# Loading positions as four rows and ordering the rotary angles around a transposed gain column

## The chip, the cores and the metric

The kernel runs on one core of one Trainium2 chip, as one launch. The metric is the device time in microseconds (us), lower is better. The engines are named as in the profile: PE is TensorE (PEld its weight load), DVE is VectorE, ACT is ScalarE, POOL is GpSimd, SP is SyncE; a q behind a name (SPq) is that engine's instruction queue where it issues a DMA.

## The reference

Two layers over 512 tokens of width 1024, all in float32. The first is a dilated attention mixer with three groups of heads, the second an mLSTM mixer; each is followed by a SwiGLU block, and a last norm ends it. What the change touches is the start of the first layer: the norm of `x`, the projections of queries and keys, and the rotary angles.

```python
def rms_norm(x, g):
    xf = x.astype(jnp.float32)
    y = xf * lax.rsqrt(jnp.mean(xf * xf, axis=-1, keepdims=True) + RMS_EPS)
    return y.astype(x.dtype) * g.astype(x.dtype)

def apply_partial_rope(t, positions):
    half = ROT_DIM // 2
    inv_freq = ROPE_THETA ** (-jnp.arange(half, dtype=jnp.float32) * 2.0 / ROT_DIM)
    ang = positions.astype(jnp.float32)[..., None] * inv_freq
    cos, sin = jnp.cos(ang)[:, :, None, :], jnp.sin(ang)[:, :, None, :]
    ...

def dilated_attention_mixer(xn, positions, w_in, w_out):
    proj = (xn @ w_in).reshape(B, S, N_GROUPS, 3, ATTN_HEADS, ATTN_HEAD_DIM)
    for g, (window, dilation) in enumerate(DIL_CONFIGS):
        q = apply_partial_rope(proj[:, :, g, 0], positions) * scale
        k = apply_partial_rope(proj[:, :, g, 1], positions)
        ...
```

`positions` is one row of 512 int32.

## The kernel before, in words

Activations lie with features on the 128 partitions and the 512 tokens along the free axis, in eight tiles. Every matmul operand is split into a high part in the reduced type `float32r` and the remainder as a low part, and three products (high times high, high times low, low times high) take the place of one full-precision product. ACT makes the high part, DVE the low part. Weights come in chunks of 512 KB on SP's DMA queue through three buffers.

The order at the start is written out by hand. The helper `behind(fn, ..., engine=E)` (L389) places what `fn` issues behind the last instruction so far on engine E, and `both` (L442) behind the last on ACT and on DVE; they set the order in which the program is laid out on each engine, and each engine then works through its own list in that order. The waits between engines follow from the data alone. The start is, in the order of the code:

- L93 to L108: constants (`cst`: identity, inverse frequencies, signs) are loaded on SP, the first norm's gains as eight rows (`attn_rows`) on POOL; DVE fills `ones`, `ones_r` and `idle_w`; PE runs nine matmuls on them (`idle(9)`) whose result is never read.
- L109, L110: ACT loads the table of the sine by a dummy activation (`warm`).
- L335 to L341: `posi` holds the positions of tokens c, c+4, c+8, ... on partition 32c, for c from 0 to 3, 128 numbers each. POOL fills the tile with 0; then four DMAs bring one row each, c = 0 and 1 issued by ACT, c = 2 and 3 by SP (L379). Each takes every fourth of the 512 integers.
- L375 to L383, on SP: four times a quarter of `x` (`x_tok`, 512 KB), and a quarter of the first weights (`first_w`, 256 KB), then two more blocks of constants. The two position DMAs stand behind the first quarter of `x`.
- `gains` (L401): PE transposes the gains (`arT`), DVE copies them to columns (`cols`).
- `rope_angles` (L346): DVE casts `posi` to `n`, spreads each partition 32c over 32 partitions (`stream_shuffle`), multiplies by the inverse frequencies, takes off whole turns (a rounding by adding and subtracting a large number, then three fused steps with a three-part two pi), and clips: nine instructions.
- `x_quarter(q)` (L446): PE transposes two tiles of `x` into PSUM (`xT`); ACT makes the high part `xa_h` with the gain as its scale (it reads `cols`), DVE the low part `xa_l`.
- `rope_tables` (L357): ACT takes the sine of the angle and of its half, DVE forms the signed sine and the cosine, POOL copies them into `sinn` and `cosn` in eight pieces. They are read by `rope_scale` (L505).
- `first_split(q)` (L416): ACT and DVE split a quarter of the first weights (`first_h`, `first_l`); `first_mm(q)` (L421) is the twelve matmuls on it.
- `x_keep` (L406): copies of the transposed `x` into the residual `h`; `squares` (L434): ACT's sums of squares for the norm.

The order in the code is: gains, angles, `x_quarter(0)`, tables, `first_split(0)`, four more idle matmuls, `first_mm(0)`, `x_keep(0)`, `x_keep(1)`, `first_split(1)`, `x_quarter(1)`, `x_quarter(2)`, `first_split(2)`, `first_mm(1)`, and so on to the ordinary loop over pairs of heads (`attention_pair`, L529, with `project`, L246).

Of the kernel before, what the change touches and what calls it, by code (L numbers as in the profile page):

```python
# [11 lines left out]
F32 = mybir.dt.float32  # L12
F32R = mybir.dt.float32r
I32 = mybir.dt.int32
AF = mybir.ActivationFunctionType
ALU = mybir.AluOpType
AX = mybir.AxisListType
P = 128

SEQ = 512  # L20
# [50 lines left out]
def tile_hybrid_dilated_attn_mlstm(  # L71
# [4 lines left out]
    nc = tc.nc  # L76
# [3 lines left out]
    def pool(stack, name, **kw):  # L80
        return stack.enter_context(tc.tile_pool(name=name, bufs=1, **kw))

    cp = pool(ctx, "const")
# [12 lines left out]
    ones = cp.tile([P, 1], F32, name="ones")  # L96
# [8 lines left out]
    def idle(n):  # L105
        for i in range(n):
            nc.tensor.matmul(idle_ps, ones_r, idle_w, start=True, stop=True)
    idle(9)  # L108
    warm = cp.tile([P, 1], F32, name="warm")  # L109
    nc.scalar.activation(warm, ones[:, 0:1], AF.Sin)  # L110
    cols = cp.tile([P, 80], F32, name="cols")
    rows = cp.tile([80 - KC, P], F32, name="rows")
    row_of = {"attn": 0}
# [45 lines left out]
    def last_on(engine):  # L159
        for ins in reversed(nc.cur_bb.bb.instructions):  # L160
            if ins.engine == engine:
                return ins
# [161 lines left out]
    with ExitStack() as actx:  # L324
        ap = pool(actx, "attn")
# [6 lines left out]
        cosn = ap.tile([R, SEQ], F32, name="cosn")  # L332
        sinn = ap.tile([R, SEQ], F32, name="sinn")
        sinr = ap.tile([R, SEQ], F32, name="sinr")
        posi = ap.tile([P, P], I32, tag="rt", name="posi", bufs=2)  # L335
        nc.gpsimd.memset(posi, 0)

        def load_positions(queue, cs):
            for c in cs:
                queue.dma_start(posi[32 * c:32 * c + 1], positions.rearrange("o (j c) -> c o j", c=4)[c])  # L340
        load_positions(nc.scalar, (0, 1))  # L341

        tmp = ap.tile([P, 2, SEQ], F32, tag="vf", name="angles")
        ang, n, sn, cs = (tmp[:, 0, i * P:(i + 1) * P] for i in range(4))

        def rope_angles():  # L346

            nc.vector.tensor_copy(n, posi)
            nc.vector.stream_shuffle(ang, n, [0] * 32)
            nc.vector.tensor_scalar(ang, ang, cst[:, K_INV:K_INV + 1], None, op0=ALU.mult)  # L350
            nc.vector.tensor_scalar(n, ang, 1.0 / TWO_PI, ROUND, op0=ALU.mult, op1=ALU.add)
            nc.vector.tensor_scalar(n, n, ROUND, None, op0=ALU.subtract)
            for c in (C1, C2, C3):
                nc.vector.scalar_tensor_tensor(ang, n, -c, ang, op0=ALU.mult, op1=ALU.add)
            nc.vector.tensor_scalar(ang, ang, math.pi, -math.pi, op0=ALU.min, op1=ALU.max)
# [19 lines left out]
        for q in range(4):  # L375
            nc.sync.dma_start(xtok[:, :, q * 256:(q + 1) * 256],
                              x.rearrange("(j c) d -> j c d", c=4)[:, :, q * 256:(q + 1) * 256])
            if q == 0:
                load_positions(nc.sync, (2, 3))  # L379
            nc.sync.dma_start(piece(raws, q).rearrange("p (k n) -> p k n", k=2),  # L380
                                w_in[q * 256:(q + 1) * 256, 0:256].rearrange("(k p) n -> p k n", p=P))
        nc.sync.dma_start(acst, consts[:, K_MA:])
# [6 lines left out]
        def behind(fn, *args, engine=mybir.EngineType.PE):  # L389

            with tc.issue_after(last_on(engine)):
                fn(*args)
# [47 lines left out]
        ACT, DVE = mybir.EngineType.Activation, mybir.EngineType.DVE  # L440

        def both(fn, *args):  # L442
            with tc.issue_after(last_on(ACT)):
                behind(fn, *args, engine=DVE)

        def x_quarter(q):  # L446
            for k in (2 * q, 2 * q + 1):
                behind(x_in, k)
        behind(gains)
        rope_angles()  # L450
        both(x_quarter, 0)
        behind(rope_tables, engine=ACT)
        both(first_split, 0)
        behind(idle, 4)
        behind(first_mm, 0)
        both(x_keep, 0)
        both(x_keep, 1)
        both(first_split, 1)
        x_quarter(1)
        x_quarter(2)  # L460
        both(first_split, 2)
# [385 lines left out]
    with ExitStack() as mctx:  # L847
# [53 lines left out]
        for p_ in (0, 32):  # L901
            s = slice(p_, p_ + H)
# [54 lines left out]
        for b in range(TB):  # L957
            s = slice(32 * b, 32 * b + H)
# [155 lines left out]
    with ExitStack() as fctx:  # L1114
# [22 lines left out]
        for n in range(2):  # L1137
# [29 lines left out]
            for at, tb, cs in tiles:  # L1167
# [12 lines left out]
                if n == 1 and cs.stop == 512:  # L1180
# [4 lines left out]
                    r = fr[:, tb:tb + 1]  # L1185
# [34 lines left out]
```

## Time and profile before

| what | us |
|---|---|
| median of 3 runs | 1482.64 |
| lowest and highest run | 1482.47, 1483.17 |
| the profiled execution | 1482.45 |
| its span | 1480.7 |
| its mean PE clock over the span | 0.998 |

The profile is of one execution. In a line of the timeline the first number is the start in us from the start of the span, the second how long the instruction, or the run of instructions merged into the line (x and their count), took; then engine, source line, operation, and the tiles written and read; in square brackets how long the engine had stood idle, and what released it. The end of a matmul is modelled, and one begins before the last has ended: the step from start to start is what tells PE's pace. In a row of stretches the first number behind the window is its length, then the busy time of PE, weight load, DVE, ACT and POOL with their instruction counts, the granted PE clock as a share of full, the busy share of the 16 DMA engines, and GB/s. A DMA row gives the size and the us from the issue to the landing.

### The profile page before, as it was taken

Reading aid. Unit: us, or ns where it says so; the run is one execution under the profiler, and the core shown is the slowest. Engines: PE = TensorE matmul, PEld = TensorE weight load, DVE = VectorE, ACT = ScalarE, POOL = GpSimd, SP = SyncE. Lnnn points to the kernel's source line nnn. Section 1 sums busy time; section 2 is a strip of 40 time slices with the busy share of each in tenths; the row PEclk is TensorE's granted clock in tenths of the full one; section 3 lists DMA queues with packets and bytes.
Section 4 is the critical chain, followed back from the end, with each engine's and each line's share of the span. In section 5 each row is a group of like instructions: output and inputs, shape, how many; then the busy total and the mean of one; then the engine's idle time right before and its main releaser. Section 6 shows DMA issues by size and latency. Waiting matters only on the chain. (4 is left out here: it accounts for less than half of the span.)

```text
span 1480.7 us, 18935 instructions
## 1 busy us (share of the span) xinstructions
PE 1469.2 (99%) x7497; PEld 1254.1 (85%) x7497; DVE 768.1 (52%) x1511; ACT 544.7 (37%) x997; POOL 104.4 (7%) x96
## 2 busy tenths in 40 slices
PE   9999999999999999999999999999999999999998
PEld 7899889889889888888888889798888888888887
DVE  6754654654665363343443338987755443443233
ACT  5334225225226342232332223785543333233223
POOL 1000000000000000111110000000000111110011
PEclk9999999999999999999999999999999999999999
DMA  6322222232132223333323333131233333333231
GB/s 185 99 86 72 82 90 72 81 92 85 58 100 80 78 86 100 100 100 100 91 88 105 94 93 88 58 100 58 74 112 92 93 99 100 100 89 96 85 100 72
DMA packets 129033, 134.45 MB, mean 91 GB/s; under 512 B 6000, under 2 KB 122032, under 8 KB 128944
## 3 DMA queue, kind: packets, MB, share of 16 engines
q1 hardware_dynamic: 126672, 131.55, 28.9%
q8 instruction: 59, 0.97, 0.3%
q10 hardware_dynamic: 1936, 1.12, 0.2%
q0 software_dynamic: 336, 0.57, 0.1%
q14 instruction: 30, 0.25, 0.1%
HBM read 131.12 MB, written 2.10 MB: 90 GB/s over the span
## 5 line engine op out<-in xcount | busy, mean ns | idle before, releaser
L241 PE MATMUL f0j<-n_h,f0j_h 128*128 128x512 f32 x352 | 137.1, 389 | 0.0
L241 PE MATMUL f1j<-n_h,f1j_h 128*128 128x512 f32 x352 | 137.1, 389 | 0.0
L241 PE MATMUL f0j<-n_h,f0j_l 128*128 128x512 f32 x352 | 137.0, 389 | 0.0
L241 PE MATMUL f1j<-n_h,f1j_l 128*128 128x512 f32 x352 | 137.0, 389 | 0.0
L241 PE MATMUL f0j<-n_l,f0j_h 128*128 128x512 f32 x352 | 136.9, 389 | 0.0
L241 PE MATMUL f1j<-n_l,f1j_h 128*128 128x512 f32 x352 | 136.9, 389 | 0.0
L211 DVE TENSOR_TENSOR f1j_l<-f1j_w,f1j_h 128x1024 fp32r<-128x1024 f32 x44 | 54.9, 1247 | 54.5 <-ACT f1j_h L210 54.5
L211 DVE TENSOR_TENSOR f0j_l<-f0j_w,f0j_h 128x1024 fp32r<-128x1024 f32 x44 | 54.8, 1245 | 54.5 <-ACT f0j_h L210 54.5
L241 PEld LDWEIGHTS f1j<-n_l,f1j_h 128*128 128x128 f32 x352 | 66.1, 188 | 13.8
L241 PEld LDWEIGHTS f0j<-n_h,f0j_h 128*128 128x128 f32 x352 | 66.1, 188 | 13.8
L241 PEld LDWEIGHTS f0j<-n_l,f0j_h 128*128 128x128 f32 x352 | 66.1, 188 | 13.7
L241 PEld LDWEIGHTS f1j<-n_h,f1j_h 128*128 128x128 f32 x352 | 66.1, 188 | 13.8
L241 PEld LDWEIGHTS f0j<-n_h,f0j_l 128*128 128x128 f32 x352 | 66.1, 188 | 13.6
L241 PEld LDWEIGHTS f1j<-n_h,f1j_l 128*128 128x128 f32 x352 | 66.1, 188 | 13.6
L210 ACT ACTIVATE f1j_h<-f1j_w 128x1024 fp32r<-128x1024 f32 x44 | 46.5, 1057 | 73.3 <-PE f1j L241 72.2
L210 ACT ACTIVATE f0j_h<-f0j_w 128x1024 fp32r<-128x1024 f32 x44 | 46.5, 1057 | 73.3 <-PE f0j L241 72.2
L1152 PE MATMUL fin<-fw_h,f1ah 128*128 128x512 f32 (+1 forms) x198 | 72.8, 368 | 0.0
L1152 PE MATMUL fin<-fw_l,f1ah 128*128 128x512 f32 (+1 forms) x198 | 72.5, 366 | 0.0
L1152 PE MATMUL fin<-fw_h,f1al 128*128 128x512 f32 (+1 forms) x198 | 72.4, 366 | 0.0
L241 PE MATMUL fo<-f0ah,fo_k_h 128*128 128x512 f32 x176 | 68.5, 389 | 0.0
L241 PE MATMUL fo<-f0al,fo_k_h 128*128 128x512 f32 x176 | 68.5, 389 | 0.0
L241 PE MATMUL fo<-f0ah,fo_k_l 128*128 128x512 f32 x176 | 68.5, 389 | 0.0
(1167 smaller groups left out, 3582.3 us busy)
## 6 DMA issues: line engine op xcount, KB each, us to landing
f0j_w<-in_ffn_w_in_dram SPq DMA_DIRECT2D x44, 512.0 KB, 3.6
f1j_w<-in_ffn_w_in_dram SPq DMA_DIRECT2D x44, 512.0 KB, 3.5
fw_w<-in_ffn_w_out_dram SPq DMA_DIRECT2D x22, 512.0 KB, 3.8
fo_k_w<-in_ffn_w_out_dram SPq DMA_DIRECT2D x20, 512.0 KB, 3.5
awo_k_w<-in_attn_w_out_dram SPq DMA_DIRECT2D x8, 512.0 KB, 3.4
mv_k_w<-in_mlstm_w_in_dram SPq DMA_DIRECT2D x8, 512.0 KB, 3.7
mqk_k_w<-in_mlstm_w_in_dram SPq DMA_DIRECT2D x8, 512.0 KB, 3.6
mo_k_w<-in_mlstm_w_in_dram SPq DMA_DIRECT2D x8, 512.0 KB, 3.7
```

The lines of the kernel that those rows point to most:

```text
L210: nc.scalar.activation(hi[:, :n], raw[:, :n], AF.Copy)
L211: nc.vector.tensor_tensor(lo[:, :n], raw[:, :n], hi[:, :n].bitcast(F32), op=ALU.subtract)
L241: nc.tensor.matmul(acc, whl[a][:, k, m * P:(m + 1) * P], pairs[b][kk], start=(kk == 0 and (a, b) == SPLITS[0]), stop=(kk == nk - 1 and (a, ...
L1152: nc.tensor.matmul(acc[i][:, cs], a[a_][kk][:, tb * P:(tb + 1) * P], whl[b_][:, k, cs], start=(kk == 0 and (a_, b_) == SPLITS[0]), stop=(k ...
```

## The change

The positions come in by one DMA that ACT issues as its first instruction: the whole row of 512 integers, four times, onto partitions 0, 32, 64 and 96. POOL's fill of the position tile goes; DVE fills the float tile `n` with 0 instead, and four casts of one partition each pick every fourth integer. The dummy sine follows the DMA on ACT.

The nine angle instructions are cut in two. `rope_turns` (zero fill, casts, shuffle, the multiplication by the frequencies, the division into turns with the rounding constant) is placed ahead of `gains`, so that on DVE it stands before the copy of `cols`; the rest, `rope_angles`, follows that copy. `rope_tables` moves from behind `x_quarter(0)` to behind `first_split(1)`.

On the engines that gives: PE, the same instructions in the same order. DVE, `memset n` behind the first memset and ahead of `ones_r`; four casts, shuffle and two scalings ahead of `cols`; the three operations of the tables behind the second `first_l` instead of ahead of the first. ACT, the DMA first of all, and the two sines behind the second `first_h` instead of ahead of the first. POOL, one memset less. SP, two DMAs less between the first quarter of `x` and the first quarter of the weights.

```diff
@@ -106,8 +106,6 @@
     idle(9)
-    warm = cp.tile([P, 1], F32, name="warm")
-    nc.scalar.activation(warm, ones[:, 0:1], AF.Sin)
     cols = cp.tile([P, 80], F32, name="cols")
@@ -332,23 +330,25 @@
-        posi = ap.tile([P, P], I32, tag="rt", name="posi", bufs=2)
-        nc.gpsimd.memset(posi, 0)
-
-        def load_positions(queue, cs):
-            for c in cs:
-                queue.dma_start(posi[32 * c:32 * c + 1], positions.rearrange("o (j c) -> c o j", c=4)[c])
-        load_positions(nc.scalar, (0, 1))
-
+
+        posi = ap.tile([P, SEQ], I32, tag="rt", name="posi", bufs=2)
+        nc.scalar.dma_start(posi.rearrange("(c r) s -> c r s", c=4)[:, 0], positions[0:1].to_broadcast([4, SEQ]))
+        warm = cp.tile([P, 1], F32, name="warm")
+        nc.scalar.activation(warm, ones[:, 0:1], AF.Sin)
         tmp = ap.tile([P, 2, SEQ], F32, tag="vf", name="angles")
         ang, n, sn, cs = (tmp[:, 0, i * P:(i + 1) * P] for i in range(4))
 
-        def rope_angles():
-
-            nc.vector.tensor_copy(n, posi)
+        def rope_turns():
+
+            nc.vector.memset(n, 0.0)
+            for c in range(4):
+                s = slice(32 * c, 32 * c + 1)
+                nc.vector.tensor_copy(n[s], posi[s].rearrange("p (j c) -> p c j", c=4)[:, c])
             nc.vector.stream_shuffle(ang, n, [0] * 32)
             nc.vector.tensor_scalar(ang, ang, cst[:, K_INV:K_INV + 1], None, op0=ALU.mult)
             nc.vector.tensor_scalar(n, ang, 1.0 / TWO_PI, ROUND, op0=ALU.mult, op1=ALU.add)
+
+        def rope_angles():
             nc.vector.tensor_scalar(n, n, ROUND, None, op0=ALU.subtract)
             for c in (C1, C2, C3):
                 nc.vector.scalar_tensor_tensor(ang, n, -c, ang, op0=ALU.mult, op1=ALU.add)
@@ -375,8 +375,6 @@
-            if q == 0:
-                load_positions(nc.sync, (2, 3))
@@ -446,16 +444,18 @@
-        behind(gains)
-        rope_angles()
+        rope_turns()
+        with tc.issue_after(last_on(DVE)):
+            behind(gains)
+        behind(rope_angles, engine=DVE)
         both(x_quarter, 0)
-        behind(rope_tables, engine=ACT)
         both(first_split, 0)
         behind(idle, 4)
         behind(first_mm, 0)
         both(x_keep, 0)
         both(x_keep, 1)
         both(first_split, 1)
+        both(rope_tables)
         x_quarter(1)
```

## The prediction

> **What bounds the kernel now.** I read the page's first part, then every wait of TensorE (PE) over the span, then the first 35 us in order of time, and last busy time by stretches. The profiled execution took 1482.45 us: a span of 1480.7 and 1.75 around it. The median of the runs, 1482.64, is 0.19 above it.
>
> ```profile
> span 1480.7 us, 18935 instructions
> PE 1469.2 (99%) x7497; PEld 1254.1 (85%) x7497; DVE 768.1 (52%) x1511; ACT 544.7 (37%) x997; POOL 104.4 (7%) x96
> ```
>
> PE is busy for 99% of the span, so the change can count only where PE stands still or runs slowly. All waits of PE (us in total, times, longest):
>
> ```profile
> PE a0g0q L428 <- ACT first_h L418: 1.9, 1, 1.9
> PE idle L107 <- DVE idle_w L102: 1.5, 1, 1.5
> PE m0s L1035 <- DVE ks L1007: 0.7, 1, 0.7
> PE m0s L1035 <- DVE m0e L1037: 0.6, 1, 0.6
> ```
>
> The change reaches the first: the first real matmul (L428) waits 1.9 us for ScalarE's (ACT's) first weight split (L418). The path to it, in order of time (start, us, engine):
>
> ```profile
> 5.66 0.27 PE L403 MATMUL arT<-cst,attn_rows 8*128 8x8 f32 x1
> ...
> 7.01 1.51 ACT L228 ACTIVATE xa_h<-xT,cols 128x512 fp32r<-128x512 f32 x2 [4.78 <-PE xT L284]
> ...
> 9.26 0.23 DVE L355 TENSOR_SCALAR angles<-angles 128x128 f32<-128x128 f32 x1
> 9.40 1.40 DVE L229 SCALAR_TENSOR_TENSOR xa_l<-xT,cols,xa_h 128x512 fp32r<-128x512 f32 x2
> ...
> 9.52 0.31 ACT L358 ACTIVATE angles<-angles 128x128 f32<-128x128 f32 x1 [1.00 <-DVE angles L355]
> 9.94 0.61 ACT L418 ACTIVATE first_h<-first_w 128x512 fp32r<-128x512 f32 x1
> 10.60 0.50 PE L428 MATMUL a0g0q<-xa_h,first_h 128*128 128x512 f32 x1 [1.88 <-ACT first_h L418]
> ...
> 11.38 0.69 DVE L419 TENSOR_TENSOR first_l<-first_w,first_h 128x512 fp32r<-128x512 f32 x1
> ...
> 15.14 1.91 PE L284 MATMUL xT<-cst,x_tok 128*128 128x128 f32 x16
> ```
>
> ACT is free at 7.01 + 1.51 = 8.52, but its next instruction in order is the sine (L358), which waits 1.00 us for the last angle on VectorE (DVE); the split stands behind it. PE's twelve matmuls then fill 10.60 to 15.14, 4.54 us. That they also run slowly is seen in stretches of 3.41 us (length; PE busy; weight load, DVE, ACT, POOL; then PE clock, DMA share, GB/s):
>
> ```profile
> 7.67:11.08 3.41, 1.53 (x7) 0.97 (x7) 3.20 (x11) 2.27 (x6) 0.02 (x1) 1.00 1.01 338
> 11.08:14.49 3.41, 3.41 (x10) 2.30 (x9) 2.75 (x6) 0.00 (x0) 3.10 (x8) 0.50 1.07 358
> 14.49:17.90 3.41, 3.38 (x24) 2.79 (x22) 1.40 (x3) 2.12 (x4) 0.17 (x1) 1.00 0.95 305
> 949.76:953.17 3.41, 2.79 (x13) 1.98 (x11) 3.32 (x6) 3.40 (x12) 0.61 (x1) 1.00 0.01 2
> 1471.95:1475.36 3.41, 2.23 (x19) 2.03 (x17) 2.04 (x9) 1.64 (x5) 1.66 (x3) 1.00 0.34 125
> 1475.36:1478.77 3.41, 0.00 (x0) 0.00 (x0) 1.10 (x5) 0.93 (x2) 0.63 (x1) 1.00 0.37 141
> 1478.77:1480.70 1.93, 0.00 (x0) 0.00 (x0) 0.00 (x0) 0.00 (x0) 0.00 (x0) 0.50 0.20 77
> ```
>
> The granted clock is exactly halved from 11.08 to 14.49, the stretch that follows one in which PE was busy for only 1.53 of 3.41 us. After stretches with 2.79 and 2.23 us busy it stays whole; after an empty one at the end it halves again. So in this trace the clock is set by stretches of 3.41 us, and the bound for halving lies between 1.53 and 2.23 busy.
>
> **The change part by part.** The program's order on PE is the same before and after; DVE gets one memset and three casts more, POOL one memset less, SP two DMAs less, ACT one DMA less.
>
> *The memset of n* now stands on DVE ahead of the idle weights, so PE's idle block and all behind it (arT, transposes, xa_h) start later. Nothing covers that: PE runs that block without a gap to arT. The row of a memset on DVE and of a 128x128 operation there (below) bound it:
>
> ```profile
> 0.74 0.39 SPq L93 DMA_DIRECT2D cst<-in_shape_constants_dram  x1
> 0.81 0.06 DVE L97 MEMSET ones<- 128x1 f32 x1 [0.81 <-PEq L1209]
> ...
> 6.84 0.23 DVE L348 CAST angles<-posi 128x128 f32<-128x128 int32 x1 [0.70 <-DMA posi<-in_positions_dram]
> 7.11 0.30 DVE L349 STREAM_SHUFFLE angles<-angles 128x128 f32<-128x128 f32 x1
> 7.44 0.28 DVE L350 TENSOR_SCALAR angles<-angles,cst 128x128 f32<-128x128 f32 x1
> 7.76 0.23 DVE L351 TENSOR_SCALAR angles<-angles 128x128 f32<-128x128 f32 x1
> 8.02 0.23 DVE L352 TENSOR_SCALAR angles<-angles 128x128 f32<-128x128 f32 x1
> ```
>
> 0 (hidden in the wait for the first memset) to 0.23; I take 0.10, nearer the memset.
>
> *The positions.* One DMA on ACT, without POOL's memset to wait for, is ACT's first instruction, so at about 0.74 like SP's first. The table load follows it; ACT has nothing else to do before 7.01, which covers both. Landing, by the nearest rows (the last number: us from issue to landing):
>
> ```profile
> attn_rows<-in_attn_norm_dram POOLq DMA_DIRECT2D x1, 4.0 KB, 3.1
> posi<-in_positions_dram ACTq DMA_DIRECT2D x1, 0.5 KB, 3.7
> first_w<-in_attn_w_in_dram SPq DMA_DIRECT2D x1, 256.0 KB, 4.6
> ```
>
> Landed at 3.8 to 4.4, and with 0.2 for the waking of DVE usable at 4.0 to 4.6. The four-row form is not in the trace; the far bound is the 4.6 of a transfer that queues, usable at 5.5. Behind this wait stand, on DVE, the casts, shuffle, two scalings, then cols (L404) and everything after it, and so ACT's xa_h, which reads cols. Four casts at a step of about 0.15 (no row has a one-row cast; 0.23 each at most), then steps of 0.33, 0.32 and 0.26 read from the rows above: cols can run 1.65 us after the positions are usable, 5.65 to 6.25. It needs arT anyway, which ends at 5.93 + 0.10 = 6.03; ACT needs cols at 7.11. Cost 0. After cols the other five angle operations take 1.5 (8.02 to 9.49 now), so the angles end at 7.7 to 7.9, just when the first xa_h does (7.01 + 0.69 + 0.10 = 7.80): xa_l is not held. It would be from about 4.6 on, and the low weight part at PE from about 4.9; later positions cost their delay, 0.6 at the far bound.
>
> *The split ahead of the sines.* xa_h ends at 8.62. The split's start against that end, its lead to PE's start, and PE's pace at full clock:
>
> ```profile
> 3.51 0.59 SPq L380 DMA_DIRECT2D first_w<-in_attn_w_in_dram  x1
> ...
> 20.72 0.48 PE L428 MATMUL a0g0q<-xa_h,first_h 128*128 128x512 f32 x1
> 21.03 0.40 PE L428 MATMUL a0g0q<-xa_l,first_h 128*128 128x512 f32 x1
> 21.05 1.27 ACT L228 ACTIVATE xa_h<-xT,cols 128x512 fp32r<-128x512 f32 x2
> 21.26 0.39 PE L428 MATMUL a0g0q<-xa_h,first_l 128*128 128x512 f32 x1
> 22.19 0.65 ACT L418 ACTIVATE first_h<-first_w 128x512 fp32r<-128x512 f32 x1
> ```
>
> There the split starts 0.13 before xa_h ends (21.05 + 1.27 against 22.19), so here at 8.49. Its weights land today at 3.51 + 4.6 = 8.1, and will land earlier with two DMAs gone from in front of them on SP. PE starts 0.66 later (10.60 - 9.94): 9.15 in place of 10.60, **1.45 us**. First use of xa_l: ready at 8.6. DVE: second xa_l from 8.66, the low part (L419) 0.66 later at about 9.3, done 10.0; PE wants it as fifth matmul at 9.15 + 0.31 + 3 x 0.23 = 10.15. No stall, 0.15 to spare.
>
> *The clock.* The idle matmuls end at 8.72 + 0.10 (of the 1.53 busy after 7.67, 0.48 lie behind 10.60), so PE now stands for about 0.3 us, not 1.9, and the stretch 7.67 to 11.08 is busy for 3.1, far over the 2.23 that kept the clock. Twelve matmuls at full clock take 0.31 + 11 x 0.228 = 2.82 instead of 4.54: **1.72 us**. The second transposes begin at 11.97 instead of 15.14.
>
> [...]
>
> *The moved sines.* On ACT (two sines), DVE (three operations, 0.7 us) and POOL (eight copies) they follow the second split, into time in which ACT and DVE wait for the second transposes. Their reader is late:
>
> ```profile
> 33.38 0.67 DVE L506 TENSOR_TENSOR sinr<-xbc,sinn 32x512 f32<-32x512 f32 x1
> ```
>
> and PE is busy throughout the stretch after the start:
>
> ```profile
> 30.00:100.00 70.00, 70.00 (x332) 58.82 (x331) 51.03 (x97) 20.59 (x35) 0.00 (x0) 1.00 0.32 98
> ```
>
> DVE ends h, h and the second low part at about 11.8 and the three by 12.5; the next xa_l needs a transposed tile (11.97 + 4 x 0.12) and 0.69 of xa_h behind it, so it cannot start before 13.1. Cover 0.6; without it their 0.7 would be on the path. POOL ends near 16, the reader comes near 30. Later loads are issued earlier too, as their buffers come free, so all behind moves with the transposes; PE has no gap there to take the gain back (70.00 of 70.00).
>
> **Sum.** 1.45 + 1.72 = 3.17, the memset's 0.10 taken off (2.4 to 3.3 with the bounds of memset and positions): 1482.45 - 3.17 = 1479.3, and by the runs' median 1479.5. That is 0.21%; 0.2% (3.0 us, about what a measurement of this kernel can tell from no change) lies just inside.
>
> **Rivals.** [...] *Positions somewhat late*, usable at 4.9 to 7.0: gain between 3.2 and nothing, middle 1481.0. *Slower: positions so late that DVE's new place makes cols the last event.* Point of decision: usable at 7.0, when cols ends at 8.8, both xa_h at 10.1, PE starts at 10.66 with the gap and the halved clock back. Each us more costs one; at a landing of 7.4 us, twice today's 3.7, they are usable at 8.3: 1483.9. Against: no small transfer took over 3.7. *The edit doesn't take effect*: the first weights, not the sine, hold ACT until 9.9; 1482.6. Against: their 4.6.
>
> **How the numbers follow.** Forecast 0.72, clock 0.10, late positions 0.08, slower 0.05, no effect 0.03, a gain over 3.5 us 0.02. Of the forecast's own range, 1479.2 to 1479.9, three quarters lie beyond 0.2%: faster 0.55 + 0.02 = 0.57; slower by over 0.2% 0.03, as it needs positions some 9 us late or another stall of that size; the rest, 0.40, within. The range 1478.8 to 1481.5 takes in the forecast, the clock and half of late positions.
>
> **What would show it.** Right: first L428 near 9.15 after a wait near 0.3; clock 1.00 in all stretches to 20 us; second transposes near 12.0; cols by 6.3; sines without a wait. Wrong: cols or xa_l waiting for the positions' DMA; first split waiting for its DMA; matmuls at 0.43; a new PE wait before 35 us.

## The result and the profile after

The changed kernel takes 1479.6 us (median of 15 runs, 1478.86 to 1479.93), the kernel before, in the same comparison, 1482.74 (15 runs, 1481.47 to 1483.65). The ratio is 0.9979, with a 95% interval of 0.9971 to 0.9987: 3.14 us or 0.21% faster. The profiled execution of the changed kernel took 1479.76, its span 1478.0.

The page's first part for the changed kernel: PE is as full as before, and its busy time is 1.4 us less for the same 7497 matmuls.

```profile
span 1478.0 us, 18932 instructions
PE 1467.8 (99%) x7497; PEld 1253.0 (85%) x7497; DVE 769.0 (52%) x1515; ACT 544.9 (37%) x997; POOL 103.4 (7%) x95
```

All waits of PE in it (us in total, times, longest). The first real matmul now waits 0.4 us instead of 1.9; the other three rows are those of before to within 0.1.

```profile
PE idle L107 <- DVE idle_w L102: 1.5, 1, 1.5
PE m0s L1035 <- DVE ks L1007: 0.7, 1, 0.7
PE m0s L1035 <- DVE m0e L1037: 0.7, 1, 0.7
PE a0g0q L426 <- ACT first_h L416: 0.4, 1, 0.4
```

The start in order of time. The positions are issued first of all and usable at 2.77; the angles are done at 7.50, ahead of the first `xa_l` (7.73); ACT goes from `xa_h` straight into the split (8.45); PE begins at 9.12 and then works without a gap to the second transposes at 11.99. The two sines (9.49 to 9.99) wait for nothing.

```profile
0.74 1.10 ACTq L335 DMA_DIRECT2D posi<-in_positions_dram  x1
2.77 1.10 DVE L346 CAST angles<-posi 1x128 f32<-1x128 int32 x4 [1.30 <-DMA posi<-in_positions_dram]
5.65 0.27 PE L401 MATMUL arT<-cst,attn_rows 8*128 8x8 f32 x1
5.96 0.17 DVE L402 COPY cols<-arT 128x8 f32<-128x8 f32 x1 [1.15 <-PE arT L401]
7.27 0.23 DVE L355 TENSOR_SCALAR angles<-angles 128x128 f32<-128x128 f32 x1
7.73 1.60 DVE L227 SCALAR_TENSOR_TENSOR xa_l<-xT,cols,xa_h 128x512 fp32r<-128x512 f32 x2 [0.23 <-ACT xa_h L226]
8.45 1.14 ACT L416 ACTIVATE first_h<-first_w 128x512 fp32r<-128x512 f32 x2
9.12 0.50 PE L426 MATMUL a0g0q<-xa_h,first_h 128*128 128x512 f32 x1 [0.35 <-ACT first_h L416]
9.25 0.68 DVE L417 TENSOR_TENSOR first_l<-first_w,first_h 128x512 fp32r<-128x512 f32 x1
9.49 0.30 ACT L358 ACTIVATE angles<-angles 128x128 f32<-128x128 f32 x1
10.17 0.40 PE L426 MATMUL a0g0q<-xa_h,first_l 128*128 128x512 f32 x1
11.99 1.91 PE L282 MATMUL xT<-cst,x_tok 128*128 128x128 f32 x16
```

The same stretches as before the change (length; PE, weight load, DVE, ACT, POOL; clock, DMA share, GB/s). The clock is whole in the stretch in which it was halved:

```profile
7.67:11.08 3.41, 3.06 (x13) 2.19 (x13) 3.25 (x6) 2.15 (x6) 0.00 (x0) 1.00 1.09 359
11.08:14.49 3.41, 3.39 (x23) 2.83 (x22) 2.41 (x7) 1.86 (x4) 2.19 (x8) 1.00 1.08 357
14.49:17.90 3.41, 3.41 (x21) 2.85 (x20) 3.38 (x6) 3.41 (x10) 0.10 (x1) 1.00 0.59 188
```

So the gain at the second transposes is 3.15 us (15.14 to 11.99). Of it, 2.7 is left in the span (1480.7 to 1478.0) and 2.69 in the profiled execution (1482.45 to 1479.76): in this pair of executions some 0.45 is lost again on the way to the end (where, the last table below shows). The medians differ by 3.14.

### The profile page after: what moved, and what is told of

Its sections match the earlier page's. It is cut to its first block, busy times and chain, and to the rows that moved or that the text cites. A ratio compares the mean times of both kernels' runs of the same rounds, so it can differ in the third digit from the quotient of the medians.

```text
span 1478.0 us, 18932 instructions
## 1 busy us (share of the span) xinstructions
PE 1467.8 (99%) x7497; PEld 1253.0 (85%) x7497; DVE 769.0 (52%) x1515; ACT 544.9 (37%) x997; POOL 103.4 (7%) x95
```

## The experiments

All were timed in five rounds (10 or 11 runs each), the first four beside one set of runs of the kernel before (median 1482.78), the last four beside another (1482.87). Two theories stood against each other at first: that the clock's halved stretch and the sine ahead of the split each carry about half of the gain, as forecast, or that one of them carries it all. Then came the question of what the early load is worth by itself.

**Fill the gap in the kernel before.** Eleven idle matmuls in place of four are to keep PE busy until the split is there; nothing else changes.

```diff
-        behind(idle, 4)
+        behind(idle, 11)
```

> The kernel before, with eleven idle matmuls in place of four between the first transposes and the first real matmul, so that PE does not stand still while it waits for the first weight split. Nothing else is moved, and the eleven end (10.4) before the split is ready (10.55). Theory: the gain has two parts, an earlier start (1.45 us) and the clock that is no longer halved (1.72). Then the first L428 stays at 10.60, the clock reads 1.00 from 11.08 to 14.49, the second transposes begin near 13.4 instead of 15.14, and the time falls by 1.7, to about 1481.0. Rival: the clock is of no account, and the time of the change comes from the earlier start and whatever else it moves; then the time stays at 1482.7.

Measured: 1481.8 (1481.27 to 1483.24), ratio 0.9993 (0.9985 to 1.0002): the median is 1.0 us less than before, not the 1.7 expected, and the interval includes 1. Ten runs end at 1481.91 at the latest, one at 1483.24. The gap was filled only in part: PE still waits 1.03 us. The first real matmul began at 10.97, not at 10.60, since the positions were usable at 7.20 in this execution and at 6.84 in that of the kernel before. The row of stretches shows the clock whole, the timeline where the rest went:

```profile
11.08:14.49 3.41, 3.09 (x13) 2.17 (x14) 3.11 (x8) 0.35 (x1) 2.79 (x7) 1.00 1.05 352
```

```profile
10.97 0.50 PE L428 MATMUL a0g0q<-xa_h,first_h 128*128 128x512 f32 x1 [1.03 <-ACT first_h L418]
11.09 0.28 DVE L360 TENSOR_SCALAR angles<-angles,cst 128x128 f32<-128x128 f32 x1
12.48 0.50 PE L428 MATMUL a0g0q<-xa_h,first_l 128*128 128x512 f32 x1 [0.32 <-DVE first_l L419]
14.44 1.91 PE L284 MATMUL xT<-cst,x_tok 128*128 128x128 f32 x16
```

At full pace PE asks for `first_l` sooner than DVE has it, since the three operations of the tables stand ahead of it (11.09 and on), and waits. The twelve matmuls take 14.44 - 10.97 = 3.47 us, not 2.82. So the whole clock alone is worth 4.54 - 3.47 = 1.07 here. Most of the other 0.65 of the forecast's 1.72 is this wait: the step from the fourth matmul to the fifth (11.77 to 12.48) is 0.71 where others are 0.23, and the one behind it 0.33. It goes only when the tables' operations leave their place ahead of `first_l`.

**Move the sines alone,** in the kernel before; positions and angles stay as they are.

```diff
-        behind(rope_tables, engine=ACT)
         both(first_split, 0)
 ...
         both(first_split, 1)
+        both(rope_tables)
```

> The kernel before with the sines, and the three operations behind them, moved behind the second weight split; positions and angles as before. Theory: the split is made at 8.5 and PE starts near 9.15, but the angles still end at 9.49 on DVE, so the second matmul waits for xa_l until 10.2 and the fifth for the low weights until 11.45. With 2.4 us busy in the stretch the clock stays whole, the second transposes begin near 13.3, and 1.8 us are gained: 1480.9; with the clock halved at 11.08 they begin near 14.9 and 0.3 is gained: 1482.4. Rival (the sines' place is all that counts): the whole gain, 1479.6.

Measured: 1481.12, ratio 0.9991 (0.9983 to 1.0), in two groups: seven runs at 1480.80 to 1481.27, four at 1482.46 to 1482.84. The profile is one of the first group (1481.08). PE's waits in it:

```profile
PE a0g0q L428 <- DVE xa_l L229: 0.9, 1, 0.9
PE a0g0q L428 <- DVE first_l L419: 0.5, 1, 0.5
PE a0g0q L428 <- ACT first_h L418: 0.5, 1, 0.5
```

The wait for ACT falls from 1.9 to 0.5, and two new ones follow, both for DVE: the late angles now hold `xa_l`, and `xa_l` holds `first_l`. The one wait became three that sum to 1.9. In place of one long gap they are spread over two stretches, with 2.14 and 2.76 of 3.41 us busy (7.01 to 10.42, 10.42 to 13.83), and in this execution neither was followed by a halved clock.

The medians hide the size, for 1481.12 lies in the lower group of this kernel and 1482.78 in the upper group of the kernel before, whose runs fall into two groups as well (below). Group against group the sines' move alone gains 0.5 in the lower (1481.00 against 1481.46) and 0.2 in the upper (1482.67 against 1482.86).

**Undo the sines' move alone,** in the changed kernel; load and angles stay early.

```diff
+        behind(rope_tables, engine=ACT)
         both(first_split, 0)
 ...
         both(first_split, 1)
-        both(rope_tables)
```

> The changed kernel with the sines back ahead of the first weight split. Theory: the angles are ready by 7.5, so the sines no longer wait and delay the split only by their own 0.42; PE starts near 9.55, DVE's three operations put the low weights at 10.65, a wait of 0.1; the clock stays whole. 0.5 is lost: 1480.1. Most of the gain is thus the early positions', not the sines' new place. Rival (the sines' place is what counts): the time is back near 1482.7.

Measured: 1479.70 (1479.46 to 1480.43), ratio 0.9983 (0.9974 to 0.9991). Its waits:

```profile
PE a0g0q L426 <- ACT first_h L416: 0.9, 1, 0.9
PE a0g0q L426 <- DVE first_l L417: 0.2, 1, 0.2
```

With the angles early the two sines cost ACT only their own time (0.39, from 7.29 to the split at 7.68). PE's wait of 0.9 can't be set beside the 0.4 of the changed kernel's profile, as PE reached its full pace earlier in this execution: the step of the idle matmuls, 0.43 from 2.11 on, shortens behind the one at 4.67, while in the changed kernel's profile it is still 0.44 at 7.47. Against the next kernel's profile, where it shortens at nearly the same time, behind the one at 4.25, the first matmul begins 0.50 later (8.36 against 7.86). The median is 0.1 above the changed kernel's 1479.6 and 0.44 above the 1479.26 of its second measurement (below), and the interval overlaps that of the whole change (0.9971 to 0.9987): once the angles are early, the sines' new place is worth at most about half a microsecond, and these runs don't separate that from nothing. The four corners, as medians; in the upper row the two values lie in different groups, so the step between them is not the worth of the sines' move:

| | sines ahead of the split | sines behind the second split |
|---|---|---|
| positions and angles late | 1482.78 | 1481.12 |
| positions and angles early | 1479.70 | 1479.6 |

**Leave a gap again, in the changed kernel:** the four idle matmuls ahead of the first real one are taken out.

```diff
-        behind(idle, 4)
```

> The changed kernel without the four idle matmuls ahead of the first real one: PE stands from about 7.8 to 9.12 and is busy for about 2.1 us of the stretch 7.67 to 11.08, between the 1.53 that was followed by the halved clock and the 2.23 that was not. The start stays at 9.12. Theory: the clock depends on the busy share of a stretch. If its bound lies above 2.1 the clock halves at 11.08, and about 1.5 us are lost (1481.1); if below, nothing is (1479.6). Rival (only an empty stretch of 3.4 us halves the clock): nothing is lost, 1479.6.

Measured: 1479.31 (1478.63 to 1479.97), ratio 0.9977 (0.9967 to 0.9986): nothing lost. The first matmul and the two stretches around it in this execution:

```profile
7.86 0.50 PE L426 MATMUL a0g0q<-xa_h,first_h 128*128 128x512 f32 x1 [1.44 <-ACT first_h L416]
```

```profile
4.53:7.94 3.41, 1.97 (x13) 1.30 (x12) 2.71 (x10) 1.79 (x3) 0.07 (x1) 1.00 1.00 327
7.94:11.35 3.41, 3.41 (x17) 2.61 (x18) 3.35 (x8) 1.03 (x3) 0.28 (x1) 1.00 1.09 355
```

PE stood for 1.44 us, and the stretch behind one with 1.97 of 3.41 us busy kept the whole clock. With the 1.53 of the kernel before, the bound for halving lies between 1.53 and 1.97 in these executions.

**The changed kernel again,** unaltered, to see what differs between executions of the same program.

> The changed kernel itself, beside the others of this call. 1479.6, and by the new theory a profile whose 3.41 us stretches may fall elsewhere against the start: PE's pace turns full between 4.5 and 7.8 in the runs so far, and up to 1.2 us of the start go with it.

Measured: 1479.26 (1478.77 to 1479.60), ratio 0.9977 (0.9968 to 0.9985). The starts differ:

```profile
5.70 1.09 PE L282 MATMUL xT<-cst,x_tok 128*128 128x128 f32 x8
8.23 0.50 PE L426 MATMUL a0g0q<-xa_h,first_h 128*128 128x512 f32 x1 [0.51 <-ACT first_h L416]
11.27 1.91 PE L282 MATMUL xT<-cst,x_tok 128*128 128x128 f32 x16
```

The first eight transposes took 1.09 us here; in the other profile of the same kernel they took 1.97, because PE was still at half its pace: from the first of them to the idle matmul behind the eighth it is 0.84 us here (5.70 to 6.54) and 1.62 there (5.85 to 7.47). The second transposes begin 0.72 earlier, and this execution was 0.69 faster (1479.07 against 1479.76).

**Early load, late turns:** the changed kernel with `rope_turns` behind the copy of `cols`.

```diff
-        rope_turns()
-        with tc.issue_after(last_on(DVE)):
-            behind(gains)
+        behind(gains)
+        behind(rope_turns, engine=DVE)
```

> The changed kernel with the whole angle computation behind the copy of cols on DVE, as before; positions still early by one DMA, sines still behind the second split. Theory (what DVE has left to do after cols sets the start): the casts begin near 6.1, the angles end near 9.6 as before the change, xa_l is late by 1.8, the low weights come near 11.6, and the second transposes begin near 13.4: 1481.1, the time of the sines moved alone (1481.1); early positions are worth nothing without the early turns. Rival (the early load itself, and SP's queue freed of two DMAs, is what counts): 1479.6.

Measured: 1482.86, ratio 1.0001 (0.9992 to 1.0009): the whole gain is gone. Again two groups, four runs at 1481.56 to 1481.61 and seven at 1482.60 to 1483.18; the expected 1481.1 is 0.5 below the first group and far from the median. Its waits and its timeline (profile of the first group):

```profile
PE a0g0q L426 <- DVE xa_l L227: 1.0, 1, 1.0
PE a0g0q L426 <- DVE first_l L417: 0.5, 1, 0.5
PE a0g0q L426 <- ACT first_h L416: 0.4, 1, 0.4
```

These are the three waits of the sines moved alone, with the same sum, and the second transposes begin at nearly the same time (13.79 and 13.76):

```profile
6.31 1.10 DVE L346 CAST angles<-posi 1x128 f32<-1x128 int32 x4
9.64 0.23 DVE L355 TENSOR_SCALAR angles<-angles 128x128 f32<-128x128 f32 x1
13.79 1.91 PE L282 MATMUL xT<-cst,x_tok 128*128 128x128 f32 x16
```

The positions have long been there, but DVE begins the casts at 6.31 and ends the angles at 9.87. That is later than the profile of the kernel before (9.26 + 0.23 = 9.49), and where the two other profiles with its load have it (9.85 with the gap filled, 9.84 with the sines alone): what DVE gains by not waiting for the positions it spends on four casts, which take 1.10 where one took 0.23. So here the early load is worth nothing by itself; it is worth something through the DVE time ahead of `cols` that it lets the turns use.

**Early turns, another load:** the changed kernel with the positions brought as the kernel before did, every fourth integer per row, but all four DMAs at the head of ACT's queue.

```diff
-        nc.scalar.dma_start(posi.rearrange("(c r) s -> c r s", c=4)[:, 0], positions[0:1].to_broadcast([4, SEQ]))
+        for c in range(4):
+            nc.scalar.dma_start(posi[32 * c:32 * c + 1, :P], positions.rearrange("o (j c) -> c o j", c=4)[c])
 ...
-                nc.vector.tensor_copy(n[s], posi[s].rearrange("p (j c) -> p c j", c=4)[:, c])
+                nc.vector.tensor_copy(n[s], posi[s, :P])
```

> The changed kernel with the positions loaded by four DMAs of every fourth integer, as before the change, but all four at the head of ACT's queue. It prices late positions, the rival on record. At 0.7 each to issue and 3.5 to land the last is usable near 6.7 instead of 2.8; cols then come near 7.9, the angles end near 9.5, the low weights near 11.5, and the second transposes begin near 13.4: 1.7 of the 3.1 gained are lost, 1481.2. If the four-row form does not matter and only the place in the queue does, the positions are there by 4.6 and the time is 1479.6.

Measured: 1484.47 (1483.84 to 1485.34), ratio 1.0013 (1.0004 to 1.0022): slower than the kernel before, and the expectation missed by 3.3 us. It took such loads to land as fast as the nearest row of the kernel before (3.7 us). The profile shows the rows usable one after the other, the last at 9.63:

```profile
3.02 0.22 DVE L347 CAST angles<-posi 1x128 f32<-1x128 int32 x1 [1.55 <-DMA posi<-in_positions_dram]
6.73 0.22 DVE L347 CAST angles<-posi 1x128 f32<-1x128 int32 x1 [3.50 <-DMA posi<-in_positions_dram]
7.55 0.22 DVE L347 CAST angles<-posi 1x128 f32<-1x128 int32 x1 [0.60 <-DMA posi<-in_positions_dram]
9.63 0.23 DVE L347 CAST angles<-posi 1x128 f32<-1x128 int32 x1 [1.86 <-DMA posi<-in_positions_dram]
10.72 0.16 DVE L403 COPY cols<-arT 128x8 f32<-128x8 f32 x1
10.98 1.27 ACT L226 ACTIVATE xa_h<-xT,cols 128x512 fp32r<-128x512 f32 x2 [6.08 <-DVE cols L403]
12.82 0.50 PE L427 MATMUL a0g0q<-xa_h,first_h 128*128 128x512 f32 x1 [4.24 <-ACT first_h L417]
```

`cols` stands behind these waits on DVE, and ACT waits 6.08 us for `cols`. PE stands 4.24 us, and the next stretch is halved:

```profile
9.82:13.23 3.41, 0.41 (x2) 0.40 (x3) 3.15 (x13) 2.25 (x5) 0.00 (x0) 1.00 1.10 352
13.23:16.64 3.41, 3.41 (x10) 2.40 (x9) 3.38 (x8) 0.46 (x3) 0.31 (x2) 0.50 0.73 240
```

This is the slower rival of the prediction, brought about by four strided loads in place of one of whole rows. Its price holds: `cols` ends at 10.88, 2.08 after the rival's point of decision (8.8), so 1482.64 + 2.08 = 1484.7, against 1484.47 measured. Why they take that long was not separated: there are four loads and not one, and each takes every fourth integer; their issue on ACT takes 2.64 us for the four; and SP's loads of `x` and weights are under way beside them.

**One idle matmul less at the head** of the changed kernel, to see whether the start of `arT` counts.

```diff
-    idle(9)
+    idle(8)
```

> The changed kernel with eight idle matmuls ahead of the gains' transpose in place of nine. PE runs that block at half pace without a gap, and the first quarter of x lands near 5.2; so arT should begin near 5.2 instead of 5.65 and everything behind it 0.3 to 0.45 earlier: 1479.2. Where the clock turns full before 5 anyway, x is the last event already and nothing is gained. Rival (the shorter block delays the full clock): the first matmuls at half pace, 1480 to 1481.

Measured: 1479.28 (1478.68 to 1479.60) beside 1479.26 of the unaltered kernel in the same comparison: no difference that can be measured. In its profile `arT` does begin earlier, at 5.23, and the second transposes at 11.59.

**All profiles together.** The second transposes' start and the time of the same execution:

| kernel | second transposes, us | execution, us | difference |
|---|---|---|---|
| gap left | 10.89 | 1478.70 | 1467.81 |
| changed, again | 11.27 | 1479.07 | 1467.80 |
| one idle matmul less | 11.59 | 1479.60 | 1468.01 |
| sines back | 11.67 | 1479.54 | 1467.87 |
| changed | 11.99 | 1479.76 | 1467.77 |
| sines alone | 13.76 | 1481.08 | 1467.32 |
| late turns | 13.79 | 1481.61 | 1467.82 |
| gap filled | 14.44 | 1481.80 | 1467.36 |
| before | 15.14 | 1482.45 | 1467.31 |
| four loads | 17.31 | 1484.63 | 1467.32 |

Over 6.4 us of starts the rest takes 1467.3 to 1468.0, so nearly all of the effect of these kernels is made before the second transposes.

The rest has an order, though. The four kernels that bring the positions by four loads take 1467.31 to 1467.36 behind the second transposes, the six that bring them by one take 1467.77 to 1468.01. That is the 0.45 which the first pair of profiles lost, and it comes with the new load: the kernel with four loads differs from the changed one only there and in what the casts read. The traces show it at two places. In the second layer, near 1020 us, the `m4s` operation on DVE waits 1.9 us for ACT's `m4j` in all six and 1.6 in all four, ACT itself stands about 0.2 us ahead of `m4j` in the six and not in the four, and in the first pair a matmul of `m6s` then starts 0.46 us behind its predecessor (1021.42 to 1021.88 in the changed kernel) where it was 0.22 (1024.55 to 1024.77 in the one before). And from the start of the last matmul to the end of the span it is 6.95 or 6.96 us in all six, 6.76 or 6.77 in all four. Why a load at the start has these two effects stays open.

## Why the prediction was right, point by point

**The time and the sum** held: 1479.5 forecast, 1479.6 measured; 3.17 us at the second transposes forecast, 3.15 measured. That the time came out to 0.1 is in part luck. The step that all behind moves with the transposes was short by 0.45: of 3.15 us the profiled pair kept 2.69. The medians still differ by 3.14, as that of the kernel before lies 0.29 above its profiled execution and that of the changed kernel 0.16 below its own. Single terms were off, and covered:

- *The memset* was taken at 0.10 and cost nothing: `arT` starts at 5.65 against 5.66. It was the lower bound of the two given; the wait ahead of the idle block is 1.52 in both.
- *The positions* were usable at 2.77, not at 4.0 to 4.6: 2.03 us after their issue began, where the nearest rows said 3.1 to 3.7. (That no small transfer took over 3.7 was misread: one of 16 KB on POOL's queue took 4.1 in the same profile.) The rows of the kernel before that carry the same tile (3.7) are strided loads and were the wrong neighbour; the four-load experiment shows how far the two forms lie apart.
- *The casts* take a step of 0.27 (1.10 for four), not 0.15, which cost 0.5. The early landing paid for it: `cols` runs when `arT` lets it (5.96), after DVE has waited 1.15 us for it, and the angles end at 7.50, ahead of the 7.7 to 7.9.
- *The split* started at 8.45 (forecast 8.49), PE at 9.12 (9.15), and the low part was there at 9.93, ahead of PE's 10.17 (10.15). The 1.45 measured 1.48.
- *The moved sines* waited for nothing. DVE ended the tables' operations at 12.39 (forecast 12.5), and then waited 0.96 for the next `xa_h`: the cover was 0.96, not 0.6.
- *The clock* was whole, and the twelve matmuls took 11.99 - 9.12 = 2.87 (2.82).

**One step was booked under the wrong name.** The forecast gave the whole 1.72 between 4.54 and 2.82 to the clock. The filled gap shows 1.07 of it to be the clock's; the other 0.65 is mostly a wait for `first_l`, hidden in the kernel before by PE's slow pace (steps of 0.43 from 11.26 to 12.12), and removed because the tables' operations left their place on DVE ahead of it. The sum came out since the change does both.

**One assumption was wrong and did no harm to the forecast.** The prediction took the boundaries of the stretches from one trace as if they were fixed to the program. They are not: the idle matmuls and transposes of the very same kernel show it (1.97 and 1.09 above). Where the boundary falls can be read from the end of the span, where PE is idle and the clock halves: at 1475.48 in the one profile of the changed kernel and at 1473.06 in the other (1.00 in the row ahead, 0.50 in the row behind).

```profile
1472.07:1475.48 3.41, 0.00 (x0) 0.00 (x0) 1.25 (x5) 1.16 (x4) 0.73 (x1) 1.00 0.36 140
1475.48:1478.00 2.52, 0.00 (x0) 0.00 (x0) 0.00 (x0) 0.00 (x0) 0.00 (x0) 0.50 0.31 121
```

```profile
1469.65:1473.06 3.41, 0.96 (x9) 0.76 (x7) 1.74 (x9) 1.50 (x5) 1.50 (x2) 1.00 0.41 156
1473.06:1476.47 3.41, 0.00 (x0) 0.00 (x0) 0.28 (x1) 0.50 (x1) 0.00 (x0) 0.50 0.40 154
```

The length of a stretch follows from the kernel before, whose clock halves at 11.05 and again at 1478.78 (the trace has the halved stretch as 3.413 us long):

```profile
11.05:14.46 3.41, 3.41 (x10) 2.30 (x9) 2.78 (x6) 0.02 (x1) 3.09 (x8) 0.50 1.07 358
1478.78:1480.70 1.92, 0.00 (x0) 0.00 (x0) 0.00 (x0) 0.00 (x0) 0.00 (x0) 0.50 0.20 76
```

1467.73 us between them are 430 stretches of 3.4133. The four-load profile has the same distance between its halvings, at 13.23 and at 1480.96. Counted back in such steps from the halving at the end, an estimate that takes the stretches as unbroken over the span, the first boundary after the span's start lies at 0.81 in the profile of before, at 0.92 and 1.91 in the two of the changed kernel, and at 3.32, 0.18, 1.36, 1.11, 0.19, 2.99 and 0.74 in the other experiments, in the order in which they stand above. That the profiles of before and after had nearly the same (0.81, 0.92) was chance.

By this estimate, whether the gap of the kernel before falls into one stretch or into two would be drawn anew in each execution, and its runs do fall into two groups: of 80 runs in the three comparisons 19 lie between 1481.31 and 1481.81 (median 1481.51) and 61 between 1482.19 and 1484.24 (median 1482.91). Against the lower group the change gains about 1.9 us (1481.51 - 1479.6), against the upper 3.3. The forecast's own base, the median of three runs (1482.64), came from the upper. All 26 runs of the changed kernel lie within 1478.77 to 1479.93. That the groups are the halved and the whole clock is read from profiles of three kernels (before halved and in its upper group; sines alone and late turns whole and in their lower groups); no two profiles of the kernel before itself, one from each group, were taken. The mean granted clock over the span, on record for 65 of the 80 runs, points the same way: 0.999 in all 15 of the lower group, 0.996 to 0.998 in 49 of the 50 of the upper. It also holds the idle end of the span, where the clock halves too, so it does not settle it alone. Of the 1.4 us between the groups the filled gap gives 1.07 to the clock; the rest stays open.

**The rivals.** The clock, for which the record holds a chance of 0.10 and a part of the range, did not halve at the start in either profile of the changed kernel: it reads 1.00 in every stretch from 7.67 to 17.90 in the first and from 7.67 to 24.72 in the second, and no run came out above 1479.93. That only an empty stretch halves the clock, the rival of the experiment with the gap, does not hold in these executions, as a stretch with 1.53 of 3.41 us busy was followed by the halved clock. Of the 1.97 us busy in the stretch from 4.53 to 7.94 of the kernel with the gap left, eight transposes make up 1.09 (5.33 to 6.42); the rest, 0.88, is less than the 1.53 that was followed by the halved clock, and the clock is whole behind it. If one bound holds for both executions, the transposes counted towards it. The slower rival did not come about in the changed kernel (usable at 2.77, decision at 7.0) but did in the four-load experiment, at its price.

## What to carry to other kernels

In this kernel a wait of 1.00 us on ACT, for an angle that DVE was still working on, held back the weight split that stood behind it, and PE with it. Look for the independent work behind such a wait, and for the engine that the wait's own producer is held by, since moving only the waiter turned one wait of 1.9 us into three of the same sum. The load brought forward gained nothing here (ratio 1.0001) until the work that reads it was also given an earlier place on its engine, and one load of whole rows was usable at 2.77 where the last of four strided ones was usable at 9.63. Where a gain hangs on the clock, price it in more than one execution, for here its boundaries moved (the halving at the end from 1475.48 to 1473.06 in one and the same kernel).

## What the runs showed of the hardware that was not expected

- The clock halved at 1475.48 in one execution of the changed kernel and at 1473.06 in another. Between the two halvings of one execution lay 1467.73 us in both profiles that show two, 430 times the 3.413 of the halved stretch. Counted back in such steps, the first boundary lies between 0.18 and 3.32 us into the span in the ten profiles, by the estimate above. The first real matmul of one and the same kernel began at 9.12 in one execution and at 8.23 in another, and the runs of the kernel before, whose profile has one gap of 1.9 us, fall into two groups 1.4 us apart.
- A stretch busy for 1.53 of 3.41 us was followed by a halved clock (0.50), one of 1.97 was not (1.00). In one execution three waits that sum to 1.9 us, spread over two stretches, left the clock whole (1.00) where it halved behind one of 1.9.
- One DMA of four whole rows was usable 2.0 us after its issue began (0.74 to 2.77), in the second profile of the same kernel 2.2 (0.74 to 2.96). Four DMAs of 512 bytes, each of every fourth integer, issued at the same place, were usable at 3.02, 6.73, 7.55 and 9.63.
- A cast of 128 numbers on a single partition lasted 0.22 us on DVE in the four-load profile, as long as one over all 128 partitions in the kernel before (0.23); the changed kernel's four, each of every fourth integer, took 0.26 each and 1.10 together.
- The six kernels with the one load are 0.41 to 0.70 us slower behind the second transposes than the four with four loads, near 1020 us and at the very end, over 1000 us behind the load.
